# Fifteen small loads behind the first three loads of a row-gradient kernel, and slots that begin at multiples of 256 bytes

## Chip, core and metric

The kernel runs on one core of a Trainium2 chip. Its time is the device time of one execution in microseconds (us); the number quoted for a kernel is the median of several executions. A profile comes from one further execution in which the hardware profiler records instructions, semaphores and every packet of the DMA engines.

## What is computed

The input `x` is an 8192 x 8192 matrix of float32 (268.44 MB), and the output has the same shape.

```python
def reference(x):
    return np.gradient(x, axis=1)
```

Along each row, an inner element becomes half the difference of its right and its left neighbour: `(x[j+1] - x[j-1]) / 2`. The first element of a row becomes `x[1] - x[0]`, and the last becomes `x[m-1] - x[m-2]`. Rows do not depend on one another. Each element is read once and written once, so 268.44 MB go in and 268.44 MB come out.

## The kernel before

**Tiling.** The 8192 rows are cut into 32 sets of 256 rows. In a set each of the 128 partitions holds two neighbouring rows (`R = 2`), which are 16384 floats, or 65536 bytes, that lie next to each other in the chip's memory (HBM). One load of a set (L60) and one store of a set (L89) are therefore one DMA each of 128 pieces of 64 KB, 8.39 MB in all. The DMAs' pieces are handled by 16 DMA engines, eight pieces each, and the trace shows a 4-byte packet per engine behind each DMA, which counts the semaphore up.

**Slots.** On-chip memory holds three slots (`NB = 3`, L40) of `SH + W` floats a partition, 64 + 16384 floats, or 65792 bytes. A set is loaded to the slot from float 64 on, and the result is written to the slot from float 0 on, so that the computation runs in place, with the output trailing the input by 64 floats. Set `i` uses slot `i % 3`. The built program places the slots, in each partition, at bytes 16512, 82304 and 148096; each of these is 128 above a multiple of 256, and so are the first bytes of what is loaded (256 further on) and of what is stored. Behind the slots lies the small tile `ends` (L41).

**One set.** Four steps follow the load: POOL (GpSimd) takes the four end differences of the two rows into `ends` (L70); DVE (VectorE) runs one custom operation over all 16382 inner floats, which subtracts and halves (L76); POOL or DVE copies the four end values into the result (L87); SP (SyncE) issues the store (L89).

**Order.** The order is written by hand (`tc.manual_schedule()`). SP issues all DMAs, in one queue and in program order: loads 0, 1, 2, and then by turns three stores and three loads: stores 0, 1, 2, loads 3, 4, 5, stores 3, 4, 5, and so on (L91 to L93). A store waits for the copy of its end values, and a load waits until the store that used its slot before has landed. `chain` (L45) declares to the scheduling layer which earlier instructions an instruction really needs, so that no others are waited for.

**Semaphores of DMAs.** In the built program the DMAs of SP's queue use eight semaphores in turn: the first DMA counts on the first semaphore, the ninth on the first again. A DMA whose semaphore has been used before carries a wait for the DMA eight places ahead of it in the queue, where that does not follow from its other waits. In the kernel before, store 3 is such a case: it waits for store 3's end values and for load 1, which has long landed then.

The lines around the issue of the DMAs are these:

```python
    with tc.manual_schedule():
        for i in range(NB):
            load(i)
        for i in range(nsets):
            ...
            ins = nc.sync.dma_start(out=out_sets[i], in_=b[:, 0:W])
            stores[i] = chain(i, ins, placed)
            if i % NB == NB - 1:
                for k in range(i + 1, min(i + 1 + NB, nsets)):
                    load(k)
```

Of the kernel before, what the change touches and what calls it, by code (L numbers as in the profile page):

```python
# [1 line left out]

# [4 lines left out]


@with_exitstack
def kernel(  # L10
    ctx: ExitStack,
    tc: tile.TileContext,
    x: bass.AP,
    out: bass.AP,
):

    nc = tc.nc
    P = nc.NUM_PARTITIONS
    n, m = x.shape
    R = 2
    NB = 3  # L30
    SH = 64
    W = R * m
    nsets = n // (P * R)
    f32 = x.dtype

    x_sets = x.rearrange("(s p t) m -> s p (t m)", p=P, t=R)
    out_sets = out.rearrange("(s p t) m -> s p (t m)", p=P, t=R)

    pool = ctx.enter_context(tc.tile_pool(name="pool", bufs=1))
    slots = [pool.tile([P, SH + W], f32, name=f"slot{k}", tag=f"slot{k}") for k in range(NB)]  # L40
    ends = pool.tile([P, nsets, R, 2], f32, name="ends", tag="ends")  # L41
    loads, stores = [], [None] * nsets
    in_front = {}

    def chain(i, ins, *needed):  # L45

        group, engine = f"slot{i % NB}", ins.ins.engine
        keep = [o.ins for o in needed]  # L50
        if in_front.get(engine, (None,))[0] == group:
            keep.append(in_front[engine][1])
        tc.declare_no_dep(ins.ins, group=group, keep=keep, reason="implied by the needed step")
        tc.add_to_no_dep_group(group, ins.ins)
        in_front[engine] = group, ins.ins
        return ins

    def load(i):
        b = slots[i % NB]
        ins = nc.sync.dma_start(out=b[:, SH : SH + W], in_=x_sets[i])  # L60
        loads.append(chain(i, ins, *([stores[i - NB]] if i >= NB else [])))

    with tc.manual_schedule():
        for i in range(NB):
            load(i)
        for i in range(nsets):
            b = slots[i % NB]
            xin = b[:, SH : SH + W].rearrange("p (t m) -> p t m", m=m)

            ins = nc.gpsimd.tensor_sub(  # L70
                out=ends[:, i, :, :],
                in0=xin[:, :, 1 : m : m - 2],
                in1=xin[:, :, 0 : m - 1 : m - 2],
            )
            at = [chain(i, ins, loads[i])]
            ins = nc.vector._custom_dve(  # L76
                dve_ops.TENSOR_TENSOR_REDUCE_SUB_MAX,
                out=b[:, 1 : W - 1],
                in0=b[:, SH + 2 : SH + W],
                in1=b[:, SH : SH + W - 2],  # L80
                s0=0.0,
                s1=0.5,
            )
            halved = chain(i, ins, *at)
            res = b[:, 0:W].rearrange("p (t m) -> p t m", m=m)
            placer = nc.gpsimd if i % 5 in (1, 3) and i < nsets - 2 else nc.vector
            ins = placer.tensor_copy(out=res[:, :, 0 : m : m - 1], in_=ends[:, i, :, :])  # L87
            placed = chain(i, ins, halved)
# [7 lines that stand above are left out]
# [1 line left out]
_INS = ['x']  # L97
_OUTS = [((8192, 8192), 'float32')]


# [23 lines left out]
```

## Time and profile before

| | |
|---|---|
| median of 3 executions | 1247.84 us (1247.62 to 1248.39) |
| span of the profiled execution, first to last instruction | 1245.7 us |
| bytes moved in the span | 536.88 MB, mean 431 GB/s |
| DVE busy | 554.6 us (45% of the span), 52 instructions |
| POOL busy | 8.8 us (1%), 48 instructions |
| DVE's custom operation (L76) | 32 times, mean 17224 ns |
| load of a set, issue to landing | median 58.0 us, 32 times |
| store of a set, issue to landing | median 40.4 us, 32 times |

The span is shorter than the median by 2.1 us, which lie around the first and last instruction or are the difference between executions. The time from issue to landing of a DMA is mostly time in line: the 16 DMA engines work through what SP has issued one after another, and two or three DMAs are in line for most of the time. The bandwidth of the span in 40 equal slices lies between 404 and 438 GB/s; the two slices at 404 GB/s are the first and the last.

### The profile page before, as it was taken

Reading aid. Unit: us, or ns where it says so; the run is one execution under the profiler, and the core shown is the slowest. Engines: PE = TensorE matmul, PEld = TensorE weight load, DVE = VectorE, ACT = ScalarE, POOL = GpSimd, SP = SyncE. Lnnn points to the kernel's source line nnn. Section 1 sums busy time; section 2 is a strip of 40 time slices with the busy share of each in tenths; the row PEclk is TensorE's granted clock in tenths of the full one; section 3 lists DMA queues with packets and bytes.
Section 4 is the critical chain, followed back from the end, with each engine's and each line's share of the span. In section 5 each row is a group of like instructions: output and inputs, shape, how many; then the busy total and the mean of one; then the engine's idle time right before and its main releaser. Section 6 shows DMA issues by size and latency. Waiting matters only on the chain.

```text
span 1245.7 us, 237 instructions
## 1 busy us (share of the span) xinstructions
DVE 554.6 (45%) x52; POOL 8.8 (1%) x48
## 2 busy tenths in 40 slices
DVE  2850583069009702850582079009603840591083
POOL 0000000000000000000000000000000000000000
DMA  9999999999999999999999999999999999999999
GB/s 404 438 436 423 427 431 438 438 438 436 436 427 431 425 438 436 425 434 436 429 434 436 434 436 434 436 434 438 419 436 436 434 438 438 431 434 429 429 410 404
DMA packets 9217, 536.88 MB, mean 431 GB/s; under 512 B 1024, under 2 KB 1024, under 8 KB 1024
## 3 DMA queue, kind: packets, MB, share of 16 engines
q1 hardware_dynamic: 9216, 536.88, 99.8%
q14 instruction: 1, 0.01, 0.0%
HBM read 268.44 MB, written 268.44 MB: 431 GB/s over the span
## 4 chain that ended last, share of the span: by engine, by line
another core or an unknown queue 74%; DVE 18%; DMA 3%; issue 2%; POOL 1%; SPq 0%; POOLq 0%
DVE slot L76 18%; DMA slot<-in_x_dram 3%; POOL ends L70 0%; POOL slot L87 0%; SPq L60 0%; POOLq L119 0%; DVE slot L87 0%
## 5 line engine op out<-in xcount | busy, mean ns | idle before, releaser
L76 DVE CUSTOM_DVE_ANT_0 slot<-slot 128x16382 f32<-128x16382 f32 x32 | 551.2, 17224 | 668.7 <-POOL ends L70 668.7
L70 POOL TENSOR_TENSOR ends<-slot 128x4 f32<-128x4 f32 x32 | 6.3, 198 | 989.6 <-DMA slot<-in_x_dram 989.6
L87 POOL COPY slot<-ends 128x4 f32<-128x4 f32 x12 | 2.3, 190 | 207.9 <-DVE slot L76 207.9
L87 DVE COPY slot<-ends 128x4 f32<-128x4 f32 x20 | 3.4, 172 | 0.7
L108 POOL MEMSET const-bfloat16-1.0<- 128x1 bf16 x1 | 0.1, 101 | 0.0
L108 POOL MEMSET const-uint8-127<- 128x1 uint8 x1 | 0.1, 101 | 0.0
L108 POOL MEMSET const-float32-0.0<- 128x1 f32 x1 | 0.1, 98 | 0.2 <-issue 0.2
L108 POOL MEMSET const-float32-1.0<- 128x1 f32 x1 | 0.1, 98 | 0.0
## 6 DMA issues: line engine op xcount, KB each, us to landing
slot<-in_x_dram SPq DMA_DIRECT2D x32, 58.0
out_dram<-slot SPq DMA_DIRECT2D x32, 40.4
```

The costliest lines, as they stand in the source:

```text
L70: ins = nc.gpsimd.tensor_sub(out=ends[:, i, :, :], in0=xin[:, :, 1 : m : m - 2], in1=xin[:, :, 0 : m - 1 : m - 2],)
L76: ins = nc.vector._custom_dve(dve_ops.TENSOR_TENSOR_REDUCE_SUB_MAX, out=b[:, 1 : W - 1], in0=b[:, SH + 2 : SH + W], in1=b[:, SH : SH + W - 2],
L87: ins = placer.tensor_copy(out=res[:, :, 0 : m : m - 1], in_=ends[:, i, :, :])
L108: nc = _bacc.Bacc("TRN2", target_bir_lowering=False, num_devices=1)
```

## The change

The diff does two things.

A tile `pad` of 32 floats (128 bytes) a partition is allocated ahead of the slots, and is never used. In the changed program the slots lie at bytes 16640, 82432 and 148224 of each partition, all multiples of 256. A tile `small` of 256 floats a partition is allocated behind the slots.

Behind loads 0, 1 and 2, and ahead of everything else in SP's queue, SP issues fifteen further loads. The k-th of them, for k from 1 to 15, brings the first 16 floats (64 bytes) of the first k rows of `x` to the first k partitions of `small`. Nothing reads `small`. These loads are not passed through `chain`.

```diff
     pool = ctx.enter_context(tc.tile_pool(name="pool", bufs=1))
+    pad = pool.tile([P, 32], f32, name="pad", tag="pad")
     slots = [pool.tile([P, SH + W], f32, name=f"slot{k}", tag=f"slot{k}") for k in range(NB)]
+    small = pool.tile([P, 16 * 16], f32, name="small", tag="small")
     ends = pool.tile([P, nsets, R, 2], f32, name="ends", tag="ends")
...
     with tc.manual_schedule():
         for i in range(NB):
             load(i)
+        for k in range(1, 16):
+            nc.sync.dma_start(out=small[0:k, 16 * k : 16 * k + 16], in_=x[0:k, 0:16])
         for i in range(nsets):
```

All else stays: the order of the 32 loads and 32 stores, what DVE and POOL do, and which of them copies which end values. Ten empty lines and three more are gone, so that line numbers are smaller: the load of a set is L49 in the changed kernel, the small loads are L56, the end differences L61, the custom operation L67, the copy L78 and the store L80.

## Prediction

> **What bounds the kernel now.** I read the page first. Its columns are busy time, share of the span and count; the DMA row gives tenths of busy time in 40 slices.
>
> ```profile
> span 1245.7 us, 237 instructions
> ...
> DVE 554.6 (45%) x52; POOL 8.8 (1%) x48
> ...
> DMA  9999999999999999999999999999999999999999
> ...
> q1 hardware_dynamic: 9216, 536.88, 99.8%
> ```
>
> The DMA engines are full in every slice, and no compute engine reaches half. So time can only come from moving faster or be lost by letting the DMA engines stand idle. The waits, of the compute engines and then of SP's queue (total us, times, longest), say the same:
>
> ```profile
> POOL ends L70 <- DMA slot<-in_x_dram: 989.6, 32, 77.4
> DVE slot L76 <- POOL ends L70: 668.7, 32, 60.2
> ```
>
> ```profile
> SPq L89 <- DVE slot L87: 525.6, 20, 55.9
> SPq L60 <- DMA out_dram<-slot: 373.1, 29, 19.3
> SPq L89 <- POOL slot L87: 300.1, 12, 36.9
> ```
>
> SP itself waits most of the time; that is free while something is in line at the DMA engines. The timeline (start, duration, line) shows how much is in line at the start:
>
> ```profile
> 0.74 1.33 SPq L60 DMA_DIRECT2D slot<-in_x_dram  x3
> 22.71 0.20 POOL L70 TENSOR_TENSOR ends<-slot 128x4 f32<-128x4 f32 x1 [22.27 <-DMA slot<-in_x_dram]
> ...
> 40.40 40.06 SPq L89 DMA_DIRECT2D out_dram<-slot  x3
> ...
> 62.44 0.20 POOL L70 TENSOR_TENSOR ends<-slot 128x4 f32<-128x4 f32 x1 [2.69 <-DMA slot<-in_x_dram]
> ...
> 81.78 39.38 SPq L60 DMA_DIRECT2D slot<-in_x_dram  x3
> ```
>
> Store 0 is issued at 40.40, while load 2 is still moving (landed 62.4, when POOL starts on it). It lands at 81.78, when SP issues load 3: 19.4 after load 2. So the engines went from load 2 to store 0 without a gap, because the store had been in line for 22 us. The steady rate comes from the chain of waits, where POOL starts on three loads that land one after another:
>
> ```profile
> 954.88 0.20 POOL ends L70
> ...
> 974.22 0.20 POOL ends L70
> ...
> 993.55 0.21 POOL ends L70
> ```
>
> One DMA of 8.39 MB takes 19.33 us. From load 0's landing (22.6) to the last landing (store 31, issued 1224.0, the shortest landing time of a store, 20.9, so 1244.9) there are 63 more: 63 x 19.33 = 1217.8, which would end at 1240.4. The other 4.5 us are lost in small pieces. The largest is at load 2, in windows that end with its landing and with store 0's (columns: length, DVE, POOL, clock, DMA share, GB/s):
>
> ```profile
> 42.00:62.40 20.40, 17.23 (x1) 0.39 (x2) 1.00 1.00 411
> 62.40:81.80 19.40, 17.40 (x2) 0.20 (x1) 1.00 1.00 432
> ```
>
> Load 2 took 20.4, so 1.07 over the steady rate, and by the packet records it is its last packet on every engine that runs about 1.1 us long.
>
> **The change: fifteen loads in SP's queue.** In the changed program's list of instructions and waits, the small loads take places 4 to 18 of the queue. With eight semaphores in turn, small loads 1 to 5 get unused ones, and from the sixth on each waits for the DMA eight places ahead: small 6 for load 0, small 7 for load 1, small 8 for load 2, small 9 for small 1, and so on to small 15 for small 7. Stores 0, 1, 2 then wait for smalls 8, 9, 10 as well as for their end values, and loads 3, 4, 5 for 11, 12, 13. SP works in order, so at small 8 it stands until load 2 has landed, and store 0, whose data are ready at 40.40, stands behind it. Store 1 (ready 59.8) stands there too; store 2 (ready 80.1) is not late. Nothing else is issued by SP; DVE and POOL wait for neither.
>
> When SP comes free the DMA lines hold no store, only small loads. I time it:
>
> 1. Load 2 lands. The row says 62.37, with the 1.07 loss, which in this trace stands at a change from load to store. With no store in line I take the steady rate: 41.98 + 19.33 = 61.3. Bounds 61.3 and 62.4.
> 2. SP issues small 8 to 15, eight DMAs. The nearest row is back-to-back issue of three loads, 1.33 us, 0.443 each. The line of single issues gives the low bound:
>
> ```profile
> L60 SPq DMA_DIRECT2D slot<-in_x_dram x32: 327/339/424, 0.7 to 1148.3; - x32
> ...
> DMA to landing us min/median/max: 21.9/58.0/60.7
> ```
>
>    8 x 0.443 = 3.5 (bounds 2.7, from 0.339, and 6.6, if all fifteen queue up behind load 2). I take 3.5: they are back to back. Small 8's own landing, which store 0 needs, is hidden in it: load 0 from empty lines took 21.9, so 2.6 more than its 19.33 of moving, and a 64-byte piece adds little.
> 3. Store 0 is issued at 61.3 + 3.5 = 64.8 and, into empty lines, lands 20.9 to 21.9 later (the shortest store, which still had something ahead of it; load 0, which had nothing). I take 21.4: 86.2, against 81.78. That is 4.4 us late.
>
> From there all is as before, moved: store 1 is 0.4 behind store 0 in line, store 2 comes at 80.1, load 3 when store 0 lands, so no further gap opens and none is won back. With the bounds the loss is 3.1 us (61.3 + 2.7 + 20.9 - 81.8) to 9.1 us (62.4 + 6.6 + 21.9 - 81.8). The fifteen loads' own bytes are 120 pieces of 64 bytes, 7.7 KB; as 64 KB pieces take 2414 ns (step between starts of neighbouring packets on one engine) and the 4-byte ones 6 ns, the at most 15 pieces an engine gets lie in the gap. If that cover were gone they would cost 15 x (about 6 + 6) = 0.2 us at packet prices. Skew that they leave between engines I put at zero, since they run ahead of store 0 in lines that are otherwise empty.
>
> **The change: slots 128 bytes further on.** DVE's and POOL's addresses move; neither bounds anything. For the DMAs the trace holds no aligned slot. A packet of 64 KB takes 2414 ns in loads and in stores alike, and a 4-byte packet 6 ns, which looks like a fixed cost a packet rather than a price of where it begins. Bounds: no gain, or two short pieces a packet (head and tail) at 6 ns each; eight packets x 64 DMAs = 512 an engine, so 0 to 6.1 us. I take zero, the like durations being the nearest row.
>
> The Trainium skill (DMA: Bandwidth & Descriptors, "How a descriptor splits into AXI transactions") speaks for a gain: a descriptor that doesn't start at a multiple of 256 bytes fetches from the boundary below, and what it doesn't use still costs beats. By it a piece here would cost 2052 beats instead of 2048, an estimate of 0.2% of the transfer time, about 2.4 us; the sum would be +2.0 instead of +4.4. The trace can't tell, as every slot is off by the same 128.
>
> **Sum.** On the profiled span: 1245.7 + 4.4 + 0 = 1250.1; the median of the runs stands 2.1 above the span, so **1252.2 us**.
>
> **Rivals.**
>
> *A. The gap opens and the 128 bytes pay.* If each packet moves 128 bytes in vain at its own rate, 128/65536 x 2414 = 4.7 ns, x 512 = 2.4 us: 1249.8. The rule of the Trainium skill named above is this one. For it: the sequence of starts is the same to the nanosecond for nearly all packets, so something rigid sets it. Against: the 4-byte packet's 6 ns already explains a fixed part.
>
> *B. The start costs more than the bytes, and the kernel gets no slower.* If a packet that begins off a boundary pays for a short head and a short tail like two 4-byte packets, 12 ns, then 512 x 12 = 6.1 us come back: 1246.1. It decides from 4.4/512 = 8.6 ns a packet on; at 13.5 ns it is faster by over 0.2%. For: nothing in the trace bounds the price above. Against: 6 ns holds the semaphore's work too.
>
> *C. The engines are set apart.* Engine by engine the small loads give different delays; if they last and keep the engines from changing from load to store at once, the rest of the 4.5 us of losses goes (3.4 without load 2's): 1248.8. Against: the spread grows without them, to 3 us between first and last engine, and losses go on.
>
> *D. The gap is larger.* Load 2 keeps its 1.07, and store 0's first packets start as slowly as load 0's (0.5 more): 1253.8; with all fifteen issues behind load 2 it is 3.1 more, 1256.9.
>
> *E. The waits do not bite*, for instance if smalls 8 to 15 pass without SP standing: store 0 still goes in line in time: 1247.8. The list of waits speaks against it.
>
> **Numbers.** Forecast 0.45, A 0.20, B 0.13, C 0.07, D 0.10, E 0.05. The bound of 0.2% (2.5 us, about what a measurement of this kernel tells from no change) lies at 1245.3 and 1250.3. Slower: 0.42 of the forecast, 0.07 of A, all of D: 0.59. Within: 0.13 of A, 0.04 of B, 0.06 of C, E, 0.03 of the forecast: 0.31. Faster: 0.09 of B and 0.01 of C: 0.10. The range goes from 1246.0 (B at 12 ns) to 1255.0 (D without the extreme issue). The forecast alone, by the bounds of the gap without the extreme issue: 1250.9 to 1253.8; the 0.03 of it that I put within 0.2% are for small losses that fall out otherwise.
>
> **What would show it.** SP waits at L56 for load 2, from about 43 to 61 or 62. Eight L56 issues back to back follow, then store 0's issue near 65. In the windows behind load 2's landing the DMA share drops for about 4 us, and load 3 is issued near 86. Steady spacing of loads of 19.33 says that alignment is worth nothing; 19.29 is A, 19.23 is B. I am wrong if store 0 is issued near 40, if the gap is under 2.5 or over 6 us, or if the spacing moves.

## The result, and the profile after

The changed kernel takes 1251.89 us in the median of five executions (1251.4 to 1252.44), the kernel before 1247.87 us beside it (1247.62 to 1248.39). The ratio is 1.0031 (95% interval 1.0021 to 1.0042): 4.0 us slower. The span of its profiled execution is 1249.5 us, 3.8 above that of before.

The page of the changed kernel, with the same rows as before:

```profile
span 1249.5 us, 257 instructions
...
DVE 554.6 (44%) x52; POOL 8.9 (1%) x48
...
DMA  9999999999999999999999999999999999999999
...
q1 hardware_dynamic: 9456, 536.88, 99.4%
```

The 20 further instructions are the fifteen issues and the extra waits; the 240 further packets are the 120 pieces of 64 bytes and a 4-byte packet behind each. At 31 us a slice the row of DMA tenths can't show what happened; the share of busy time in the queue's row, 99.8% before and 99.4% now, just does. The waits of SP's queue name the place:

```profile
SPq L80 <- DVE slot L78: 481.1, 19, 55.9
SPq L49 <- DMA out_dram<-slot: 378.1, 29, 19.8
SPq L80 <- POOL slot L78: 280.2, 11, 36.7
SPq L56 <- DMA slot<-in_x_dram: 57.0, 3, 19.0
```

The last row is new: the issue of a small load waits three times for the load of a set, 19 us each. Before, SP stood that long for DVE's and POOL's end values, which cost nothing, since the stores went in line in time; 20 such waits on DVE have become 19. The timeline of SP's DMA issues and of POOL's first steps says when it was free again (start, duration, issues merged):

```profile
0.74 1.32 SPq L49 DMA_DIRECT2D slot<-in_x_dram  x3
2.10 62.23 SPq L56 DMA_DIRECT2D small<-in_x_dram  x15
...
64.44 14.99 SPq L80 DMA_DIRECT2D out_dram<-slot  x3
...
85.26 19.67 SPq L49 DMA_DIRECT2D slot<-in_x_dram  x2
```

```profile
61.36 2.97 SPq L56 DMA_DIRECT2D small<-in_x_dram  x8
61.41 0.20 POOL L61 TENSOR_TENSOR ends<-slot 128x4 f32<-128x4 f32 x1 [1.59 <-DMA slot<-in_x_dram]
```

Load 2 landed just ahead of 61.36. Then SP issued eight small loads in a row, and only at 64.44 store 0, which before was issued at 40.40. It landed by 85.26, when load 3 is issued, against 81.78. In the stretch between (columns: length, DVE, POOL, clock, DMA share, GB/s) the engines move 1 GB/s:

```profile
61.34:64.44 3.10, 2.80 (x1) 0.20 (x1) 1.00 0.02 1
```

So far that is 3.5 us. How far the landing of each load of a set (POOL's start on it) lies behind the kernel before is in this table, worked out from the two timelines, in us:

| | store 0 landed | load 3 | load 5 | load 8 | load 20 | load 31 |
|---|---|---|---|---|---|---|
| changed kernel | 3.5 | 4.3 | 5.1 | 5.0 | 4.3 | 3.7 |

The loss doesn't stay as it was at store 0: it grows by 0.8 up to load 3 and by another 0.8 up to load 5, and part of it is won back later. In the chain of waits of the changed kernel, loads 3, 4 and 5 are these:

```profile
144.17 0.21 POOL ends L61
...
163.49 0.20 POOL ends L61
...
183.82 0.20 POOL ends L61
```

In the kernel before they are these:

```profile
139.89 0.21 POOL ends L70
...
159.25 0.20 POOL ends L70
...
178.70 0.20 POOL ends L70
```

In the changed kernel it is 19.32 from load 3 to load 4 and 20.33 from load 4 to load 5, 1.0 over the steady rate. In the kernel before load 5 came 19.45 after load 4. That is where the DMAs change from loads to stores, as at load 2 of the kernel before, which had its 20.4 there. The step up to load 3 stands at the change ahead of it, from stores to loads. In the packet records it is again the last packets that run long: those of store 2 by 0.7 us in the mean of the engines (by nothing in the kernel before), those of load 5 by 0.9 us (0.2 before).

### The profile page after: what moved, and what is told of

Same layout as the page of the kernel before. It is cut to its first block, busy times and chain, and to the rows that moved or that the text cites. A ratio compares the mean times of both kernels' runs of the same rounds, so it can differ in the third digit from the quotient of the medians.

```text
span 1249.5 us, 257 instructions
## 1 busy us (share of the span) xinstructions
DVE 554.6 (44%) x52; POOL 8.9 (1%) x48
## 3 DMA queue, kind: packets, MB, share of 16 engines
q1 hardware_dynamic: 9456, 536.88, 99.4%
## 4 chain that ended last, share of the span: by engine, by line
another core or an unknown queue 74%; DVE 18%; DMA 3%; issue 2%; POOL 1%; SPq 0%; POOLq 0%
DVE slot L67 18%; DMA slot<-in_x_dram 3%; POOL ends L61 0%; POOL slot L78 0%; SPq L49 0%; POOLq L110 0%; DVE slot L78 0%
## 5 line engine op out<-in xcount | busy, mean ns | idle before, releaser
L67 DVE CUSTOM_DVE_ANT_0 slot<-slot 128x16382 f32<-128x16382 f32 x32 | 551.2, 17224 | 672.4 <-POOL ends L61 672.4
L61 POOL TENSOR_TENSOR ends<-slot 128x4 f32<-128x4 f32 x32 | 6.4, 200 | 993.2 <-DMA slot<-in_x_dram 993.2
L78 POOL COPY slot<-ends 128x4 f32<-128x4 f32 x12 | 2.3, 192 | 207.9 <-DVE slot L67 207.9
L78 DVE COPY slot<-ends 128x4 f32<-128x4 f32 x20 | 3.4, 172 | 0.7
```

The source lines that it names most:

```text
L61: ins = nc.gpsimd.tensor_sub(out=ends[:, i, :, :], in0=xin[:, :, 1 : m : m - 2], in1=xin[:, :, 0 : m - 1 : m - 2],)
L67: ins = nc.vector._custom_dve(dve_ops.TENSOR_TENSOR_REDUCE_SUB_MAX, out=b[:, 1 : W - 1], in0=b[:, SH + 2 : SH + W], in1=b[:, SH : SH + W - 2],
```

## The experiments

All times are medians; "before" is the kernel before beside them, 1248.04 (27 executions), 1248.03 (17) and 1248.07 (11) in the three groups of runs. Diffs are against the changed kernel. Two things were open: whether the place of the slots does anything, and whether the gap is made by standing, by issuing or by the small loads' own traffic.

**Slots alone.**

```diff
-        for k in range(1, 16):
-            nc.sync.dma_start(out=small[0:k, 16 * k : 16 * k + 16], in_=x[0:k, 0:16])
```

> The tiles pad and small stay, so the slots lie at multiples of 256 bytes; the fifteen loads are left out. Gap theory (all the loss is SP standing ahead of store 0): as before, 1247.9 us, with store 0 issued at 40.4 and loads landing 19.33 apart. Slots theory A (128 bytes saved a packet): 1245.4 and a spacing of 19.29. Theory B (two short pieces saved): 1241.8 and 19.23. If the slots' new place costs something: above 1248.5.

Measured: 1246.99 us (1246.59 to 1248.73, 11 executions), ratio 0.9994 (0.9986 to 1.0003). Store 0 is issued in time:

```profile
40.26 40.25 SPq L78 DMA_DIRECT2D out_dram<-slot  x3
```

The loss belongs to the loads: the same kernel with them, the changed one, takes 4.9 us more (in another group of runs). The interval holds "no change", but the median lies 1.05 below before, between my reading and theory A.

**Loads alone.** The same fifteen loads, with the slots 128 bytes off again.

```diff
-    pad = pool.tile([P, 32], f32, name="pad", tag="pad")
```

> The fifteen loads stay, pad is left out, so the slots lie 128 bytes above a multiple of 256 again. Gap theory: as the changed kernel, 1251.9, store 0 issued at 64.4 and landed at 85.2. Slots theory A (the slots won 2.4 and the loads cost 6.4): 1254.3.

Measured: 1253.05 us (1252.75 to 1253.35), ratio 1.0041 (1.0029 to 1.0054), 5.0 above before and 1.2 above the changed kernel. Store 0 was issued at 64.41 and had landed at 85.25, just as in the changed kernel. The expected 1251.9 was missed by as much as the slots alone had seemed to gain, so this was tried again below.

**The fifteen in fives.** Five behind loads 0 to 2, five behind stores 0 to 2, five behind loads 3 to 5, where the waits by turn of semaphores ask for nothing that the DMA doesn't need anyway.

```diff
-        for k in range(1, 16):
-            nc.sync.dma_start(out=small[0:k, 16 * k : 16 * k + 16], in_=x[0:k, 0:16])
+        def few(first):
+            for k in range(first, first + 5):
+                nc.sync.dma_start(out=small[0:k, 16 * k : 16 * k + 16], in_=x[0:k, 0:16])
+        few(1)
...
             if i % NB == NB - 1:
+                if i == 2:
+                    few(6)
                 for k in range(i + 1, min(i + 1 + NB, nsets)):
                     load(k)
+                if i == 2:
+                    few(11)
```

> The same fifteen loads and the same slots as in the changed kernel, but five behind loads 0 to 2, five behind stores 0 to 2 and five behind loads 3 to 5; no semaphore of a small load's or a store's wait then belongs to a set's load or store that the DMA still needs to bring, so SP never stands for it. Gap theory: store 0 issued at 40.4 again and 1247.9 (at most 0.3 for the fifteen loads' own packets). Rival (the small loads themselves cost, by their short packets or by setting the engines apart): 1251.9 as with all fifteen, or below 1246 if setting the engines apart helps (rival C).

Measured: 1247.18 us (1246.92 to 1247.85, 11 executions), ratio 0.9995 (0.9986 to 1.0004). SP's queue, in the timeline:

```profile
2.11 1.68 SPq L57 DMA_DIRECT2D small<-in_x_dram  x5
40.47 39.95 SPq L83 DMA_DIRECT2D out_dram<-slot  x3
80.47 1.72 SPq L57 DMA_DIRECT2D small<-in_x_dram  x5
82.24 39.05 SPq L49 DMA_DIRECT2D slot<-in_x_dram  x3
```

Load 3 is issued half a microsecond later than before, while stores 1 and 2 are in line. It also lands 0.5 later, but of that 0.3 is left at load 31 against the slots alone, and the same fifteen loads with the same slots are 0.2 us above the slots alone in the medians. So where SP never stands for a DMA of a set, neither the small loads' traffic nor a step that they leave between the engines makes a loss of 4 us: the loss goes with where SP stands.

**Seven of the fifteen.**

```diff
-        for k in range(1, 16):
+        for k in range(1, 8):
```

> Only the first seven of the fifteen loads, slots at multiples of 256. Store 0 now carries the wait for load 2 itself, with nothing to issue ahead of it. Gap theory with the eight issues as its price: store 0 issued at 61.4 and landed 20.8 later, 82.2, so 0.4 later than before: 1248.3. Rival (standing until load 2 has landed is the price, and the issues are small beside it): store 0 lands at 84 or later, 1250 to 1252.

Measured: 1249.04 us (1248.47 to 1249.81, 11 executions), ratio 1.0009 (1.0000 to 1.0017). The times of the queue are as expected to the tenth:

```profile
2.11 40.20 SPq L56 DMA_DIRECT2D small<-in_x_dram  x7
61.40 18.01 SPq L80 DMA_DIRECT2D out_dram<-slot  x3
82.25 19.65 SPq L49 DMA_DIRECT2D slot<-in_x_dram  x2
```

Standing until load 2 has landed, by itself, makes store 0 land 0.5 later than before: the start of the store from empty lines is lost (0.9 us from its issue to its first packet, 62.28, in the packet records), but load 2 lands 1.0 earlier with no store behind it. The rest of the changed kernel's 3.5 at this place is the eight issues. The whole kernel is 1.0 slower, though, not 0.4: load 3 is 1.25 behind the kernel before and load 5 2.0, the same two steps of about 0.8 as above. The expected 1248.3 missed them.

**Twenty-three loads.**

```diff
-        for k in range(1, 16):
-            nc.sync.dma_start(out=small[0:k, 16 * k : 16 * k + 16], in_=x[0:k, 0:16])
+        for k in range(1, 24):
+            r = min(k, 15)
+            nc.sync.dma_start(out=small[0:r, 16 * k : 16 * k + 16], in_=x[0:r, 0:16])
```

(`small` is made 24 x 16 floats wide.)

> Twenty-three loads instead of fifteen (the last eight of 15 rows), slots at multiples of 256. Gap theory with the issues as its price: sixteen instead of eight are issued behind load 2, 0.38 us each, so store 0 is issued at 64.4 + 3.1 = 67.5 and lands at 88.3: 1251.9 + 3.1 = 1255.0. Rival (a wait of a fixed length, for load 2 and one small load's landing): as with fifteen, 1251.9. Rival (each further eight also waits for the eight ahead to land, 2.4 us more): store 0 near 69.9, 1257.4.

Measured: 1255.94 us (1254.82 to 1256.76), ratio 1.0060 (1.0047 to 1.0072).

```profile
2.10 65.69 SPq L57 DMA_DIRECT2D small<-in_x_dram  x23
67.91 11.43 SPq L81 DMA_DIRECT2D out_dram<-slot  x3
```

Eight more issues put store 0 back by 3.5 us and the time by 4.0. The last eight have 15 rows each, where the eight before have 8 to 15, and take longer to issue: 0.43 from one to the next instead of 0.385. The time is 0.9 above the expected one. Neither a fixed wait nor one of 2.4 us more fits.

**One row each.**

```diff
-            nc.sync.dma_start(out=small[0:k, 16 * k : 16 * k + 16], in_=x[0:k, 0:16])
+            nc.sync.dma_start(out=small[0:1, 16 * k : 16 * k + 16], in_=x[0:1, 0:16])
```

> Fifteen loads as in the changed kernel, but each of one row, so that the 1-to-15 step over the engines is gone. Gap theory: only the number of issues counts, store 0 issued at 64.4 within 0.5, 1251.9 within 0.7. Rival C (the step between the engines matters, to the good or the bad): the time moves by over 1 us.

Measured: 1251.41 us (1250.56 to 1252.86, 7 executions), ratio 1.0027 (1.0016 to 1.0038). The time is in the expected half microsecond, the place is not: store 0 is issued at 63.56, 0.9 earlier. Of this 0.2 is load 2, which landed that much sooner here, and 0.7 the eight issues behind it, 2.4 us instead of 3.1. The durations of the issues (min/median/max in ns) say why, first in this kernel and then in the changed one:

```profile
L56 SPq DMA_DIRECT2D small<-in_x_dram x15: 222/251/445, 2.1 to 63.2; - x15
```

```profile
L56 SPq DMA_DIRECT2D small<-in_x_dram x15: 245/301/443, 2.1 to 63.9; - x15
```

An issue is not one price: behind load 2 it takes SP longer the more rows a small load has. Without any step over the engines the kernel is as slow as with it, within the intervals; rival C is out.

**Behind the stores.** The two lines of the loop are moved to `if i == 2:` behind store 2.

> The same fifteen loads behind stores 0 to 2 instead of behind loads 0 to 2, slots at multiples of 256. By the turn of eight semaphores small load 6 waits for store 0, the seventh for store 1 and the eighth for store 2, and load 3 stands behind them all. Gap theory: SP stands at L82 until store 2 has landed (120.8), issues eight loads in 3.1 us, load 3 is issued at 123.9 instead of 81.8 and lands near 145.4 instead of 139.8: 5.2 to 6.0 lost at that place, 1252.3 to 1253.8. If it is only loads that must not be waited for: 1247.5.

Measured: 1253.93 us (1253.65 to 1254.35), ratio 1.0045 (1.0032 to 1.0058).

```profile
80.45 42.87 SPq L82 DMA_DIRECT2D small<-in_x_dram  x15
123.36 1.33 SPq L49 DMA_DIRECT2D slot<-in_x_dram  x3
145.46 0.20 POOL L59 TENSOR_TENSOR ends<-slot 128x4 f32<-128x4 f32 x1 [82.87 <-DMA slot<-in_x_dram]
```

Here SP stands for store 2 instead of load 2, and the same gap opens in front of load 3, which lands 5.6 later than before, 22.0 after its issue. Whether a load or a store is waited for makes no difference to that; in both kernels it is the last one in line. The end is 0.1 above the expected range; load 5 is 6.8 behind, so this kernel too lost 1.2 at the next changes.

**Slots 4 bytes off**, without small loads.

```diff
-    slots = [pool.tile([P, SH + W], f32, name=f"slot{k}", tag=f"slot{k}") for k in range(NB)]
+    slots = [pool.tile([P, 64 + SH + W], f32, name=f"slot{k}", tag=f"slot{k}")[:, 1 : 1 + SH + W] for k in range(NB)]
...
-        for k in range(1, 16):
-            nc.sync.dma_start(out=small[0:k, 16 * k : 16 * k + 16], in_=x[0:k, 0:16])
```

> No small loads; each slot begins 4 bytes above a multiple of 256, which is neither a multiple of 32 nor of 64. My reading (the price of a packet does not depend on where it begins): the step between packets stays 2414 ns, loads land 19.33 apart, time as with the slots alone, 1247.0 to 1248.0. Slots theory A or B: 2.4 us or more above that, 1249.4 and up. If short pieces are rounded up to 32 bytes only: one more 32-byte unit in 2052, 0.6 us, 1247.6 to 1248.6.

Measured: 1247.75 us (1246.31 to 1248.73, 11 executions), ratio 0.9996 (0.9988 to 1.0005). The most common step between packets is 2414 ns in its packet records, as in those of every kernel here. The time also lies in the range expected if short pieces were rounded up, 1247.6 to 1248.6, so the time alone does not tell the two apart; a price on every packet would show in the common step, and doesn't.

**The slots' place once more, with the fifteen loads**: the changed kernel again, the loads alone again, and the fifteen loads with slots 4 bytes off (the edit of `slots` above).

> The changed kernel itself, beside the next two, to see what the slots' place is worth on one chip in one sitting. Gap theory: 1251.9 and all three within 0.5. If slots at multiples of 256 are worth the 1.2 us by which the loads alone came out slower: this one 1251.9, the next two 1253.

> The fifteen loads without pad, slots 128 bytes above a multiple of 256, once more. Gap theory: within 0.5 of the changed kernel beside it. Slots worth something: 1.0 or more above it. The step between packets is 2414 ns either way.

> The fifteen loads, slots 4 bytes above a multiple of 256. Gap theory: within 0.5 of the changed kernel beside it. Slots worth something by their place: as with 128 bytes off or worse.

| slots begin | median, range | ratio | store 0 landed, load 8, load 31 behind before |
|---|---|---|---|
| at multiples of 256 | 1251.58 (1251.43 to 1252.82) | 1.0028 (1.0018 to 1.0039) | 3.3, 5.1, 3.7 |
| 128 above | 1252.87 (1252.53 to 1254.01) | 1.0040 (1.0027 to 1.0052) | 3.4, 5.6, 5.5 |
| 4 above | 1253.60 (1252.88 to 1254.10) | 1.0044 (1.0031 to 1.0056) | 3.4, 5.1, 5.9 |

The intervals of the ratios overlap, though every execution with slots 4 above took longer than every one with slots at multiples of 256. In all five pairs (these two, the loads alone against the changed kernel, and without loads the slots alone against before and against 4 off) the kernel with slots at multiples of 256 is the faster one, by 0.8 to 2.0 (two of the pairs are from different groups of runs). The table shows that in the profiled executions it isn't won in the gap, but between load 8 and load 31. That holds for every profile here: from load 8 to load 31 the nine profiles with slots at multiples of 256 gain 0.4 to 2.9 us on the kernel before, small loads or not, and of the four others, with slots 128 or 4 bytes above, three gain 0.1 at most and one loses 0.8 (the table's last row). I take the slots' place as worth about 1 us, likely though not settled.

The packet records show a part of the means. The common packet takes the same time everywhere (2418 ns, and 2414 from start to start), but not equally many do: 7645 to 7819 of the 8192 packets with slots at multiples of 256, 7150 to 7299 with slots 128 above, 6311 and 6437 with slots 4 above. What the others take longer, without the packets that run long by 60 ns and more, most of them at the start and at the changes, adds up to 0.1 to 0.2, 0.3 to 0.5 and 0.6 us an engine. The rest of the 1 us stays open.

**Half of the engines set back.** Behind the fifteen, three loads of 8 partitions and 11264 bytes.

```diff
+        for k in (16, 24, 32):
+            nc.sync.dma_start(out=small[k : k + 8, :], in_=x[k : k + 8, 0:2816])
```

(`small` is made 2816 floats wide.)

> The changed kernel with three more loads behind the fifteen, of 8 partitions and 11264 bytes each, so that half of the engines come to store 0 some 0.6 us later than the other half. Three more issues: store 0 issued at 65.5 and landed near 86.9. The kernels with a gap lost 0.8 us more at load 3 and 0.8 more at load 5 than the kernel before. Theory (they do because the gap puts the engines in step, so that all of them change direction at once): these two losses shrink, load 5 ends up less than 1.0 later against store 0's landing than before the change, and the time is 1251.9 + 1.1 + 0.6 - 0.8 = 1252.8. Rival (a change of direction behind a gap costs that whatever the engines' step): load 5 is 1.6 later again, 1253.6.

Measured: 1253.65 us (1252.99 to 1254.80), ratio 1.0045 (1.0032 to 1.0059).

```profile
65.60 13.98 SPq L82 DMA_DIRECT2D out_dram<-slot  x3
88.94 38.91 SPq L49 DMA_DIRECT2D slot<-in_x_dram  x3
```

Store 0 landed 23.3 after its issue instead of 20.8, so the setback was 2.5 us and not 0.6, and the expected times don't apply. Behind the kernel before it is 7.2 at store 0, 6.9 at load 3, 7.7 at load 5 and 5.4 at load 31. The step at load 3 is gone, the one up to load 5 is not, and load 6 is another 0.8 behind, at 8.5. From store 0 to load 6 this kernel loses 1.4 us more than the kernel before, just as the changed kernel does. So it is not borne out that the gap's further cost comes from engines in step; what it comes from stays open.

## Why the prediction came out right

The forecast was 1252.2 us and the measured time 1251.89. The main step holds, but that the sum is only 0.3 off is luck: misses of both signs met.

- **The wait, and what stands behind it.** Right. SP stood at L56 for loads 0, 1 and 2, and store 0 behind it; the fives show that the same loads without that standing cost about nothing.
- **Load 2's landing at 61.3.** Right: 61.36 is SP's next issue. With no store in line, load 2 doesn't lose its 1.07.
- **Eight issues, 3.5 us.** The right term, mis-sized by 0.4: 61.36 to 64.44 is 3.1. The row I took, three issues of 128 rows, was the nearest but dearer one.
- **Store 0 from empty lines, 21.4 us.** 20.8, just under the low bound of 20.9. With the issues the loss at this place is 3.5 instead of 4.4.
- **"From there all is as before, moved."** This step failed. In each of the kernels that stand for load 2 with only the fifteen (or fewer or more) small loads, the next two changes between stores and loads lose 0.7 to 1.0 each that the kernel before doesn't lose (where the small loads stand behind the stores it is 1.2 up to load 5; with three larger loads behind the fifteen, 0.5 up to load 5 and 0.8 more up to load 6). Why they do is open.
- **Small loads' own packets at nothing.** Right, by the fives: 0.2 us against the slots alone, with ranges that overlap.
- **Slots at zero.** Likely wrong by about 1 us: the loads alone cost 5.0 and 4.8 us in two groups, the two parts together 4.0 and 3.5. What the changed kernel wins back behind load 5, from 5.1 to 3.7, is likely this too: with the slots where they were nothing is won back, and the loads alone are 5.3 and 5.4 behind the kernel before at load 5, and 5.4 and 5.5 at load 31. Rival A's price, 2.4 us by the packets' pace, is not it either. The Trainium skill's rule (DMA: Bandwidth & Descriptors, "How a descriptor splits into AXI transactions") would make pieces shorter that begin at a multiple of 256. The packet records show 2414 ns as the common step with slots 0, 4 and 128 bytes above one, so this case does not bear it out in the pace of packets. The sign I set for it, a spacing of loads of 19.29 instead of 19.33, was too fine: spacings near 19.3 differ by some hundredths from one stretch to the next.
- **Rival D's extra 1.07** did not occur; **E** falls by SP's three waits at L56.

In terms of the profiles, then: 3.5 us at the gap and 1.6 at the next two changes of direction, together the 5 us that the loads cost by themselves; then some 1.4 less by the end, likely the slots' part, which makes 3.7 at load 31. The forecast had 4.4 and nothing.

## What to carry to other kernels

A DMA's price is not only its bytes: it takes a place in its queue and a semaphore from a small set, and by the turn of semaphores it can make everything behind it wait for a DMA that it has nothing to do with. Before adding DMAs, list for each which DMA's semaphore it inherits, and ask whether, when that wait ends, anything is still in line at the DMA engines; with five loads at a time 0.2 us was lost here, within the noise, with fifteen at once about 5 us for the same slots. In a kernel bound by transfers an interruption need not be won back (here it was not, with the slots left in place), and its cost can go on growing behind the place where it shows.

## What the hardware showed unexpectedly

- A load's last packets run long when a store is in line behind it: load 2 took 20.4 us with store 0 waiting and landed 1.0 us earlier without. At later changes from loads to stores the kernel before loses between nothing and 0.6 us in the mean of the engines.
- The time SP takes to issue a small DMA grows with its rows: a median of 251 ns for one row each; behind load 2 of the changed kernel 272 ns for 8 rows, rising one by one to 382 ns for 15. A DMA of 128 rows takes 327 to 424 ns, so the growth does not go on. Rows are not all: behind the stores, the loads of 4, 5 and 6 rows took 569 to 578 ns each.
- The common step of 64 KB packets on an engine, 2414 ns, is the same for loads and stores and for slots 0, 4 or 128 bytes above a multiple of 256. But with slots at multiples of 256 fewer packets depart from the common duration: 373 to 547 of 8192, against 893 to 1042 at 128 above and 1755 to 1881 at 4 above.
- None of the kernels run beat the kernel before beyond its interval; the slots alone came nearest, at 0.9994 (0.9986 to 1.0003).
